# Level matmuls of a gated linear recurrence and value products of attention in column tiles of TensorE, and a later tanh

## Chip, core and metric

The kernel runs on one core of one Trainium2 chip. The metric is the device time of one execution in microseconds. A core has five engines with instruction streams of their own: TensorE (PE in the profile; its weight loads are PEld), VectorE (DVE), ScalarE (ACT), GpSimd (POOL) and SyncE (SP). Matmuls write to PSUM, which has eight banks here; everything else lives in SBUF.

## The reference

Two layers of an encoder trunk work on 512 positions of 1024 channels. Each layer normalises x, makes one wide input projection, runs three branches on it, merges them with gates, and ends with an MLP. What the change touches is in branch A and branch C:

```python
def step(state, inp):                       # branch A, chunks of positions, per head
    qt, kt, vt, bt = inp                    # bt: running sum of the log forget gates
    diff = bt[:, :, :, None, :] - bt[:, :, None, :, :]
    decay = jnp.exp(jnp.where(tri[:, :, None], diff, -jnp.inf))
    attn = jnp.einsum('nhtk,nhsk,nhtsk->nhts', qt, kt, decay)
    o_intra = jnp.einsum('nhts,nhsv->nhtv', attn, vt)
...
y_a = (rms_norm(o_a, a_norm[l]) * jax.nn.silu(a_g.astype(jnp.float32).reshape(o_a.shape)))
...
o = jnp.einsum('bnhgqk,bnkhd->bnqhgd', p.astype(v.dtype), vb)   # branch C, values
```

Branch A has 4 heads of 128 channels and runs forwards and backwards. Branch C is attention in a band of three blocks of 128 keys, with 8 query heads on 2 key and value heads of 64 channels.

## The kernel before, in words

All matrices are fp32. The big products are split into a rounded high and a low part and done as three matmuls (lines 268 to 270, 319 to 321, 532 to 534, 566 to 568). Weights come in chunks of 128x1024; ACT casts each chunk to its high part (`wh`, line 262) and DVE subtracts to get the low part (`wl`, line 263).

A layer has a stage in which branch A's heads, branch C and the remaining projections run beside each other. Python code gives the order of creation and priorities (`hp`, `later`, `overlap`); the scheduler of the framework then orders each engine's instructions by them and by its own estimate of times. `tc.issue_after(i)` holds an instruction back until `i` has been placed.

Branch A, `a_head`: the decay between positions t and s of a chunk is worked out by levels, L = 1, 2, 4, 8, 16, 32, 64. At a level the positions fall into blocks of L, and the decay between two neighbouring blocks is a product of a factor for the query (`qt`) and one for the key (`kt`), both made by an Exp on ACT from the running sums `ex`, which DVE extends level by level (line 775). So a level's share of the 128x128 matrix `at` (per group of 128 positions, of which there are four) is a plain product of `kt` and `qt`, right where the two blocks are neighbours and meaningless elsewhere. `attn` computes the whole 128x128 product for four groups into a PSUM tile of 128x512 (four matmuls, line 734). For L = 1 the tile is copied as it is (ACT, line 754); for L = 2 to 16 `put` copies it under a mask of the right entries (DVE, line 739, masks in `amask_t`), with one more product for the diagonal itself (`key` times `q`) at L = 2; for L = 32 and 64 the blocks off the diagonal are copied (ACT, line 767). In all there are 8 calls of `attn` for a head, and 4 heads in each of 2 layers. After the levels come the states (lines 779 to 807) and the product of `at` with the values (`av`, line 819).

Branch C, `c_out`: for a pair of heads `j` and a block of queries `n` the probabilities are transposed (`pT`, line 1209) and multiplied with the values `cv` (line 1214). The value tile has the 64 channels of both heads side by side, so one matmul per key block computes both heads' queries (256 columns) against both heads' channels (128 rows), and half of the result is used: two copies of 64 partitions (line 1216) take the right halves to `yc`.

`gate_a` projects branch A's output gate, scales it, and makes its SiLU from a tanh (lines 1109 to 1113) as soon as it can. The four gates are multiplied into branch A's heads at line 1280, ahead of the product `yA`. Branch C's `yc` is split into high and low parts (`yh`, line 327, and `yl`) ahead of the product `yC`.

Of the kernel before, what the change touches and what calls it, by code (L numbers as in the profile page):

```python
# [8 lines left out]
U8 = mybir.dt.uint8  # L9
# [3 lines left out]
P = 128  # L13
# [16 lines left out]
def ap_of(t, off, dims):  # L30
    return bass.AP(tensor=t.tensor, offset=t.offset + off, ap=[t.ap[0]] + dims)
# [47 lines left out]
def trunk(tc, x0v, xT, xt, ws, fnb, bsb, snk, wst, rope, cmask, amask, ident, out):  # L79
    nc = tc.nc  # L80
# [35 lines left out]
    def T(tag, name, dt=F32):  # L116
        where = part[HOME[tag]] if tag in HOME else sb
        return where.tile([P, S], dt, tag=tag, bufs=SLOTS[tag], name=nm(name))
# [161 lines left out]
    def proj(xs, name, *key, bank="m"):  # L280

        return proj_w(xs, name, wload(*key), bank=bank)
# [443 lines left out]
    def a_head(l, h, ex, q, vt, oa):  # L726

        at = part["br"].tile([P, 4, P], F32, tag="at", bufs=2, name=nm("at"))

        def attn(kk, qq):  # L730
            pt = PT("a", "at")
            for st in range(4):
                c = slice(st * P, (st + 1) * P)
                nc.tensor.matmul(pt[:, c], kk(st), qq[:, c], start=True, stop=True)  # L734
            return pt

        def put(pt, mi):
            mk = ap_of(amask_t, mi * P, [[0, 4], [1, P]])
            nc.vector.copy_predicated(at, mk, pt.rearrange("p (a b) -> p a b", a=4))

        X, R, Y, PP = 0, S, 2 * S, 3 * S
        for li, L in enumerate(LEVELS):
            nb = 256 // L
            shp = "p (b h i) -> p b h i"
            e_k = ap_of(ex, 0, [[2 * L, nb], [2 * S + L, 2], [1, L]])
            e_q = ap_of(ex, S, [[2 * L, nb], [2 * S + L, 2], [1, L]])
            qt = T("a", "qt")
            nc.scalar.activation(qt.rearrange(shp, b=nb, h=2), e_q, AF.Exp)  # L748
            nc.vector.tensor_tensor(qt, qt, q, ALU.mult)
            kt_ = T("a", "kt")  # L750
            nc.scalar.activation(kt_.rearrange(shp, b=nb, h=2), e_k, AF.Exp)
            if L == 1:
                pt = attn(lambda st: kt_[:, st * P:(st + 1) * P], qt)
                at_copy[0] = nc.scalar.copy(at, pt.rearrange("p (a b) -> p a b", a=4))
                dg = Z2("key")[:, 0]
                nc.scalar.activation(dg.rearrange(shp, b=nb, h=2), ap_of(ex, 2 * S, [[2, nb], [1 - 2 * S, 2], [1, 1]]), AF.Exp)
                nc.vector.tensor_tensor(dg, dg, kt_, ALU.add)
            else:
                pt = attn(lambda st: kt_[:, st * P:(st + 1) * P], qt)
                if L < 32:  # L760
                    put(pt, li)
                    if L == 2:
                        put(attn(lambda st: dg[:, st * P:(st + 1) * P], q), 0)
                else:
                    for r in range(0, P, L):
                        o = r ^ L
                        nc.scalar.copy(at[r:r + L, :, o:o + L], ap_of(pt[r:r + L], o, [[P, 4], [1, L]]))  # L767

            d = [[2 * L, nb], [1, L]]
            z = [[2 * L, nb], [0, L]]
            for o_, ostep, i_, istep in ((X, PP + L - X, PP + 2 * L - 1, -L), (Y + L, R - Y - L, R, L)):
                o_ap = ap_of(ex, o_, [[ostep, 2]] + d)
                nc.vector.tensor_tensor(o_ap, o_ap, ap_of(ex, i_, [[istep, 2]] + z), ALU.add)  # L775
            yield
# [130 lines left out]
    for l in range(DEPTH):  # L907
# [127 lines left out]
        begin("Y1")  # L1035
        begin("br")
        if l == 0:
            amask_t = cst.tile([P, 7 * P], U8, name="amask_t")
            for i in range(2):
                w = slice(i * 448, (i + 1) * 448)  # L1040
                am = T("a", "am")
                nc.sync.dma_start(am[:, 0:448], amask[:, w])
                nc.vector.tensor_copy(amask_t[:, w], am[:, 0:448])
            snk_t = const(bass.AP(tensor=snk.tensor, offset=snk.offset, ap=[[0, P], [1, 16]]), [P, 16], name="snk_t")
            nc.vector.tensor_scalar(snk_t, snk_t, -1.0, None, ALU.mult)
        cmask_t = part["br"].tile([P, 3 * P], F32, tag="cmask", bufs=1, name=nm("cmask"))
# [59 lines left out]
        sg = []  # L1106

        def gate_a():
            z = evac(proj(xs, "ag", l, "ag", len(sg)), "l2", "ag")
            th = T("jk", "th")  # L1110
            nc.scalar.activation(th, z, AF.Tanh, scale=0.5)
            nc.vector.scalar_tensor_tensor(z, th, 1.0, z, ALU.add, ALU.mult)
            sg.append(z)


        for t, view in ((cos_t, natural), (sin_t, sorted_)):
# [82 lines left out]
        def c_out(j, n, lo_, nb, Ps):  # L1199
# [11 lines left out]
            po = PT("s", "po")  # L1211
            for b in range(nb):
                kb = (lo_ + b) * P
                nc.tensor.matmul(po[:, 0:2 * P], cv[:, kb:kb + P], pT[:, b].rearrange("p a b -> p (a b)"), start=b == 0, stop=b == nb - 1)  # L1214
            for h, r in enumerate((lo64, hi64)):
                nc.scalar.copy(yc[j][r, n * P:(n + 1) * P], po[r, h * P:(h + 1) * P])

        def gates(tag, i, fl):

# [37 lines left out]
        with later(30000):  # L1257
            for h in range(4):
                gate_a()

            ys = y_split(yc, "yh")
            kept = []
            for fl in range(2):
                th = gates("ch", 0, fl)
# [273 lines left out]
def _host(x, w_in, ln1, lb_logits, a_norm, w_s, b_s, sink, w_br, w_out, ln2, w_up, w_down, final_norm):  # L1538
# [28 lines left out]
    cm[:, 2 * P:] = np.where(j <= i, 0.0, NEG)  # L1567
    a["cmask"] = cm
    am = [i == j]
    for L in LEVELS[1:7]:  # L1570
        am.append((i // (2 * L) == j // (2 * L)) & (i // L != j // L))
    a["amask"] = np.concatenate(am, axis=1).astype(f)
    a["ident"] = np.eye(P, dtype=f)
    return a

# [22 lines left out]
```

## Time and profile before

| what | value |
|---|---|
| median of 3 runs | 1606.75 us (1604.58 to 1606.84) |
| the profiled execution | 1605.07 us |
| its span | 1603.3 us |
| share of the clock granted to TensorE | 0.997 |
| stage of the mixers, layer 0 | about 160 to 430 us |
| stage of the mixers, layer 1 | about 978 to 1226 us |

The page gives the busy time of each engine, and the chain of work that ended last, followed back from the last instruction. Groups of instructions are given as line, engine, operation, tile written and tiles read, shapes, count, and then busy time, mean duration in ns, and the idle time of the engine just before them with the instruction that ended it. A timeline row gives the start, the time up to the end of the last one of a merged row, and a count; an engine's idle time before it stands in brackets. An fp32 matmul of the program is two records in the profile.

### The profile page before, as it was taken

How to read it: one execution, taken by the hardware profiler on the slowest of the kernel's cores; microseconds unless marked ns; L12 is line 12 of the kernel's file. 1: busy time of each engine (PE TensorE's matmuls, PEld its weight loads, DVE VectorE, ACT ScalarE, POOL GpSimd, SP SyncE). 2: the span in 40 equal slices, each digit the busy share in tenths (PEclk: the TensorE clock that was granted, in tenths of full speed). 3: DMA queues.
4: the chain of work that ended last, by engine and by line, in shares of the span. 5: the costliest groups of instructions: out<-in, count | busy, mean ns of one | idle time of the engine just before them, and what ended most of it. 6: DMA issues, size and time to landing. Idle time of an engine off the chain costs nothing.

```text
span 1603.3 us, 24656 instructions
## 1 busy us (share of the span) xinstructions
PE 1574.3 (98%) x9186; PEld 1420.6 (89%) x9186; DVE 1312.3 (82%) x1980; ACT 1065.4 (66%) x1819; POOL 185.1 (12%) x249
## 2 busy tenths in 40 slices
PE   9999999999999999999999999999999999999997
PEld 8887889899889999999888888799998898989896
DVE  7876898785677989797997769998856789797988
ACT  7667668686337848576876766688763477576675
POOL 1020000000231110100211100000003210110101
PEclk9999999999999999999999999999999999999999
DMA  9764321222485776866745742222225767867644
GB/s 348 196 164 128 123 74 65 89 96 92 154 293 158 190 194 182 200 182 178 191 132 172 219 137 82 79 73 86 86 87 203 244 187 193 205 174 201 173 110 112
DMA packets 74152, 250.55 MB, mean 156 GB/s; under 512 B 9168, under 2 KB 9552, under 8 KB 74032
## 3 DMA queue, kind: packets, MB, share of 16 engines
q1 hardware_dynamic: 45216, 156.03, 28.0%
q0 software_dynamic: 24064, 84.29, 24.0%
q10 hardware_dynamic: 4752, 8.65, 1.5%
q8 instruction: 72, 1.18, 0.3%
q14 instruction: 48, 0.39, 0.1%
HBM read 230.07 MB, written 18.87 MB: 155 GB/s over the span
## 4 chain that ended last, share of the span: by engine, by line
PE 79%; DVE 10%; ACT 5%; issue 3%; DMA 2%; POOL 1%; POOLq 0%; DVEq 0%; ACTq 0%
PE blks L534 3%; PE blks L533 3%; PE blks L532 3%; PE blkc L566 3%; PE blkc L567 3%; PE blkc L568 3%; DVE wl L263 3%; PE blka L534 2%; PE blka L533 2%; PE blka L532 2%; PE at L734 2%; PE po L1214 2%; PE blka L566 2%; PE blka L567 2%; PE blka L568 2%
## 5 line engine op out<-in xcount | busy, mean ns | idle before, releaser
L263 DVE TENSOR_TENSOR wl<-wr,wh 128x1024 fp32r<-128x1024 f32 x166 | 202.5, 1220 | 77.0 <-ACT wh L262 68.3
L262 ACT CAST wh<-wr 128x1024 fp32r<-128x1024 f32 x166 | 173.7, 1047 | 129.9 <-PE yA L320 27.9
L263 DVE TENSOR_TENSOR wl<-t,wh 128x1024 fp32r<-128x1024 f32 x158 | 192.0, 1219 | 52.2 <-ACT wh L262 51.6
L262 ACT CAST wh<-t 128x1024 fp32r<-128x1024 f32 x158 | 165.1, 1046 | 101.5 <-PE blks L533 24.0
L262 ACT CAST wh<-b 128x1024 fp32r<-128x1024 f32 x91 | 94.9, 1043 | 49.9 <-PE blks L533 14.0
L263 DVE TENSOR_TENSOR wl<-b,wh 128x1024 fp32r<-128x1024 f32 x91 | 110.6, 1219 | 16.0 <-ACT wh L262 15.4
L252 POOL DMA_DIRECT2D t<-in_ws_dram x72 | 65.4, 918 | 376.9 <-DMA t<-in_ws_dram 210.9
L533 PE MATMUL blks<-wh,sl 128*128 128x512 f32 x256 | 96.5, 380 | 1.2 <-DVE sl L328 1.2
L532 PE MATMUL blks<-wh,sh 128*128 128x512 f32 x256 | 93.3, 379 | 0.0
L534 PE MATMUL blks<-wl,sh 128*128 128x512 f32 x256 | 90.9, 381 | 0.2 <-DVE wl L263 0.2
L775 DVE TENSOR_TENSOR ex<-ex 128x512 f32<-128x512 f32 x112 | 78.9, 721 | 0.2
L328 DVE TENSOR_TENSOR sl<-u,sh 128x512 fp32r<-128x512 f32 x112 | 75.0, 682 | 2.0 <-ACT sh L327 2.0
L567 PE MATMUL blkc<-xl,wh 128*128 128x256 f32 x256 | 70.1, 275 | 0.0
L566 PE MATMUL blkc<-xh,wh 128*128 128x256 f32 x256 | 70.0, 275 | 0.0
L327 ACT CAST sh<-u 128x512 fp32r<-128x512 f32 x112 | 67.5, 614 | 3.6 <-DVE u L631 3.6
L568 PE MATMUL blkc<-xh,wl 128*128 128x256 f32 x256 | 69.6, 275 | 0.0
L252 POOL DMA_DIRECT2D wr<-in_ws_dram x32 | 28.0, 874 | 340.6 <-DVE t L501 92.8
L734 PE MATMUL at<-qt,kt 128*128 128x128 f32 x448 | 65.4, 276 | 1.7 <-DVE ex L775 1.5
L748 ACT ACTIVATE qt<-ex 128x512 f32<-128x512 f32 x56 | 37.6, 672 | 42.5 <-DVE ex L775 26.1
L734 PEld LDWEIGHTS at<-qt,kt 128*128 128x128 f32 x448 | 59.5, 192 | 4.2 <-ACT at L767 2.3
L533 PEld LDWEIGHTS blks<-wh,sl 128*128 128x128 f32 x256 | 48.4, 189 | 8.8 <-DVE sl L328 2.0
L534 PEld LDWEIGHTS blks<-wl,sh 128*128 128x128 f32 x256 | 48.4, 189 | 8.2 <-DVE wl L263 1.6
(444 smaller groups left out, 5316.7 us busy)
## 6 DMA issues: line engine op xcount, KB each, us to landing
wr<-in_ws_dram SPq DMA_DIRECT2D x134, 512.0 KB, 3.7
b<-in_ws_dram SPq DMA_DIRECT2D x91, 512.0 KB, 5.4
t<-in_ws_dram POOLq DMA_DIRECT2D x72, 512.0 KB, 8.3
t<-in_ws_dram SPq DMA_DIRECT2D x58, 512.0 KB, 4.4
wr<-in_ws_dram POOLq DMA_DIRECT2D x32, 512.0 KB, 5.6
thd<-zt ACTq DMA_DIRECT2D x32, 256.0 KB, 4.5
th<-thd POOLq DMA_DIRECT2D x32, 256.0 KB, 3.7
mgd<-mg POOLq DMA_DIRECT2D x16, 256.0 KB, 2.5
```

The source lines that it names most:

```text
L252: nc.gpsimd.dma_start(self.t[what][i], self.chunk(q, i), accum_op=ALU.add)
L262: cast_i[0] = nc.scalar.copy(hi, raw)
L263: sub_i[0] = nc.vector.tensor_tensor(lo, raw, hi.bitcast(F32), ALU.subtract)
L328: return nc.vector.tensor_tensor(lo, src, hi.bitcast(F32), ALU.subtract)
L532: nc.tensor.matmul(o, xh[:, t], h, start=start and k == 0, stop=False, skip_group_check=True)
L533: nc.tensor.matmul(o, xl[:, t], h, start=False, stop=False, skip_group_check=True)
L534: i = nc.tensor.matmul(o, xh[:, t], l_, start=False, stop=k == 3, skip_group_check=True)
L566: nc.tensor.matmul(o, hl[0][:, c], xh, start=start and k + j == 0, stop=False, skip_group_check=True)
L567: nc.tensor.matmul(o, hl[0][:, c], xl, start=False, stop=False, skip_group_check=True)
L568: i = nc.tensor.matmul(o, hl[1][:, c], xh, start=False, stop=k == 3, skip_group_check=True)
L734: nc.tensor.matmul(pt[:, c], kk(st), qq[:, c], start=True, stop=True)
L775: nc.vector.tensor_tensor(o_ap, o_ap, ap_of(ex, i_, [[istep, 2]] + z), ALU.add)
```

## The change

The level products of branch A are computed only in the blocks that are used. `attn` now takes a width `w`: for each of the four groups it makes 128 / w matmuls, each with w columns of `kt` as weights and w columns of `qt` (or `q`) as moving data. The result, w by w, goes to partitions r to r + w, which are also the column tile of TensorE (`tile_position=(0, r)`); the four groups lie side by side, so the PSUM tile has 4w columns. For L up to 16 and for the diagonal w is 32, and the results, the 32x32 blocks on the diagonal, are collected in the first 32 columns of `at` (`diag`). L = 32 and L = 64 take their blocks off the diagonal straight, with w = L. At L = 32 the three diagonal blocks below the first are copied to their places first. The masks shrink to 32 columns each, with 5 in place of 7.

Branch C's value products are made head by head: 64 columns of `cv` as weights, 128 queries as moving data, output at partitions 0 to 63 or 64 to 127 in the same 128 columns. One copy takes the result to `yc`.

The tanh of the output gates, and the product behind it, move from `gate_a` to a function `silu` that is called after `yc` has been split, and are held back until the last cast of that split (`halves_i[0]`) has been placed.

```diff
+        diag = at[:, :, 0:32]
+
-        def attn(kk, qq):
+        def attn(k_, q_, w, other):
+
             pt = PT("a", "at")
             for st in range(4):
-                c = slice(st * P, (st + 1) * P)
-                nc.tensor.matmul(pt[:, c], kk(st), qq[:, c], start=True, stop=True)
-            return pt
+                for r in range(0, P, w):
+                    k0 = st * P + r
+                    q0 = st * P + (r ^ w if other else r)
+                    nc.tensor.matmul(pt[r:r + w, st * w:(st + 1) * w], k_[:, k0:k0 + w], q_[:, q0:q0 + w], start=True, stop=True, tile_position=(0, r), skip_group_check=True)
+            return pt[:, 0:4 * w].rearrange("p (a b) -> p a b", a=4)
 
         def put(pt, mi):
-            mk = ap_of(amask_t, mi * P, [[0, 4], [1, P]])
-            nc.vector.copy_predicated(at, mk, pt.rearrange("p (a b) -> p a b", a=4))
+            nc.vector.copy_predicated(diag, ap_of(amask_t, mi * 32, [[0, 4], [1, 32]]), pt)
...
             if L == 1:
-                pt = attn(lambda st: kt_[:, st * P:(st + 1) * P], qt)
-                at_copy[0] = nc.scalar.copy(at, pt.rearrange("p (a b) -> p a b", a=4))
+                at_copy[0] = nc.scalar.copy(diag, attn(kt_, qt, 32, False))
...
+            elif L < 32:
+                put(attn(kt_, qt, 32, False), li)
+                if L == 2:
+                    put(attn(dg, q, 32, False), 0)
             else:
-                pt = attn(lambda st: kt_[:, st * P:(st + 1) * P], qt)
-                if L < 32:
-                    put(pt, li)
-                    if L == 2:
-                        put(attn(lambda st: dg[:, st * P:(st + 1) * P], q), 0)
-                else:
-                    for r in range(0, P, L):
-                        o = r ^ L
-                        nc.scalar.copy(at[r:r + L, :, o:o + L], ap_of(pt[r:r + L], o, [[P, 4], [1, L]]))
+                pt = attn(kt_, qt, L, True)
+                if L == 32:
+                    for r in range(32, P, 32):
+                        nc.scalar.copy(at[r:r + 32, :, r:r + 32], diag[r:r + 32])
+                for r in range(0, P, L):
+                    nc.scalar.copy(at[r:r + L, :, r ^ L:(r ^ L) + L], pt[r:r + L])
...
-            amask_t = cst.tile([P, 7 * P], U8, name="amask_t")
-            for i in range(2):
-                w = slice(i * 448, (i + 1) * 448)
-                am = T("a", "am")
-                nc.sync.dma_start(am[:, 0:448], amask[:, w])
-                nc.vector.tensor_copy(amask_t[:, w], am[:, 0:448])
+            amask_t = cst.tile([P, 5 * 32], U8, name="amask_t")
+            am = T("a", "am")[:, 0:5 * 32]
+            nc.sync.dma_start(am, amask)
+            nc.vector.tensor_copy(amask_t, am)
...
         def gate_a():
-            z = evac(proj(xs, "ag", l, "ag", len(sg)), "l2", "ag")
+            sg.append(evac(proj(xs, "ag", l, "ag", len(sg)), "l2", "ag"))
+
+        def silu(z, after):
             th = T("jk", "th")
-            nc.scalar.activation(th, z, AF.Tanh, scale=0.5)
+            with tc.issue_after(after.ins):
+                nc.scalar.activation(th, z, AF.Tanh, scale=0.5)
             nc.vector.scalar_tensor_tensor(z, th, 1.0, z, ALU.add, ALU.mult)
-            sg.append(z)
...
             for b in range(nb):
                 kb = (lo_ + b) * P
-                nc.tensor.matmul(po[:, 0:2 * P], cv[:, kb:kb + P], pT[:, b].rearrange("p a b -> p (a b)"), start=b == 0, stop=b == nb - 1)
-            for h, r in enumerate((lo64, hi64)):
-                nc.scalar.copy(yc[j][r, n * P:(n + 1) * P], po[r, h * P:(h + 1) * P])
+                for h, r in enumerate((lo64, hi64)):
+                    nc.tensor.matmul(po[r, 0:P], cv[:, kb + h * 64:kb + (h + 1) * 64], pT[:, b, h], start=b == 0, stop=b == nb - 1, tile_position=(0, h * 64), skip_group_check=True)
+            nc.scalar.copy(yc[j][:, n * P:(n + 1) * P], po[:, 0:P])
...
             ys = y_split(yc, "yh")
+            for z in sg:
+                silu(z, halves_i[0])
```

The scheduler then places the instructions anew. Three places show it. The first is PE in layer 0, where head 0 reaches its last two levels, beside the projection `gz` (a merge gate). Before:

```order
L269 MATMUL gz_2078<-xl_193,wh_2074 128x512
L734 MATMUL at_1477<-qt_1472,kt_1475 128x128 x4
L270 MATMUL gz_2078<-xh_192,wl_2075 128x512
L268 MATMUL gz_2078<-xh_196,wh_2074 128x512
L269 MATMUL gz_2078<-xl_197,wh_2074 128x512
```

The same place after the change:

```order
L270 MATMUL gz_2215<-xh_188,wl_2212 128x512
L739 MATMUL at_1546<-qt_1541,kt_1544 32x32 x10
L739 MATMUL at_1577<-qt_1572,kt_1575 64x64 x8
L739 MATMUL at_1546<-qt_1541,kt_1544 32x32 x6
L268 MATMUL gz_2215<-xh_192,wh_2211 128x512
```

Where one level stood as four wide matmuls, 16 narrow ones of L = 32 now stand with the 8 of L = 64 in their midst.

The second place is PE a little later, where head 0 ends with its product `av` while head 1 is at its level L = 8. Before:

```order
L819 MATMUL av_1972<-vt_677,at_1397 128x128
L734 MATMUL at_2133<-qt_2128,kt_2131 128x128
L819 MATMUL av_1972<-st_1845,qd_1849 128x128
L734 MATMUL at_2133<-qt_2128,kt_2131 128x128
L819 MATMUL av_1972<-st_1882,qd_1886 128x128
```

After:

```order
L821 MATMUL av_2108<-vt_677,at_1394 128x128
L739 MATMUL at_2270<-qt_2265,kt_2268 32x32
L821 MATMUL av_2108<-st_1945,qd_1949 128x128
L739 MATMUL at_2270<-qt_2265,kt_2268 32x32
L821 MATMUL av_2108<-st_2006,qd_2010 128x128
```

The alternation was there already, between products of one shape; now full and narrow matmuls take turns. In the whole of PE's new order there are 896 matmuls of 32x32, 64 of 64x64 and 160 of 64x128, and neighbours differ in output width (128, 64 or 32) 440 times.

The third place is ACT at the end of layer 1's stage, around the split of the last `yc`. Before:

```order
L1111 ACTIVATE th_11912<-ag_11910 128x512
L834 ACTIVATE on_11593<-oT_11588,x0v_t 128x512
L1216 COPY yc_11356<-po_11507 64x128 x2
L1111 ACTIVATE th_11948<-ag_11946 128x512
L327 CAST yh_11963<-yc_11356 128x512
L262 CAST wh_12165<-wr_12163 128x1024
```

After:

```order
L836 ACTIVATE on_12366<-oT_12361,x0v_t 128x512
L1218 COPY yc_12080<-po_12275 128x128
L327 CAST yh_12724<-yc_12080 128x512
L1114 ACTIVATE th_12728<-ag_12611 128x512
L1114 ACTIVATE th_12731<-ag_12644 128x512
L262 CAST wh_12938<-wr_12936 128x1024
```

The four tanh (`th`) now follow the cast `yh`, two of them ahead of the next weight cast.

More of the change, by code (lines that the diff above doesn't have):

```diff
@@ L1569, in _host @@
     am = [i == j]
-    for L in LEVELS[1:7]:
+    for L in LEVELS[1:5]:
         am.append((i // (2 * L) == j // (2 * L)) & (i // L != j // L))
-    a["amask"] = np.concatenate(am, axis=1).astype(f)
+    a["amask"] = np.concatenate([np.concatenate([m[r:r + 32, r:r + 32] for r in range(0, P, 32)]) for m in am], axis=1).astype(f)
     a["ident"] = np.eye(P, dtype=f)
```

## The prediction

> **What bounds the kernel now.** I read the page first: the busy times, then the chain that ended last.
>
> ```profile
> span 1603.3 us, 24656 instructions
> PE 1574.3 (98%) x9186; PEld 1420.6 (89%) x9186; DVE 1312.3 (82%) x1980; ACT 1065.4 (66%) x1819; POOL 185.1 (12%) x249
> ...
> PE 79%; DVE 10%; ACT 5%; issue 3%; DMA 2%; POOL 1%; POOLq 0%; DVEq 0%; ACTq 0%
> ```
>
> TensorE (PE) is busy in 98% of the span and holds 79% of the chain. So a matmul that goes away is worth nearly its own share of PE's stream, unless another engine is just behind. Next come the windows of the two mixer stages (one per layer) in which branches A and C run, and, inside each, the stretch where PE has gaps.
>
> ```profile
> core 0: us, PE busy (x) PEld busy (x) DVE busy (x) ACT busy (x) POOL busy (x), PEclk, DMA share, GB/s
> 160.00:430.00 270.00, 264.40 (x1488) 236.57 (x1487) 212.22 (x420) 184.55 (x404) 17.04 (x27) 0.99 0.26 90
> 978.00:1226.00 248.00, 241.63 (x1371) 216.73 (x1370) 202.73 (x408) 175.16 (x390) 17.24 (x27) 1.00 0.24 85
> ...
> 180.00:240.00 60.00, 56.43 (x314) 49.61 (x314) 59.44 (x105) 42.17 (x78) 1.10 (x2) 1.00 0.23 80
> 1000.00:1040.00 40.00, 36.07 (x207) 31.84 (x206) 37.66 (x71) 26.18 (x56) 1.11 (x2) 1.00 0.21 76
> ```
>
> Over a whole stage VectorE (DVE) has room: 212.2 of 270 us and 202.7 of 248. Only in the two short stretches is it full (59.4 of 60, 37.7 of 40), and there PE stands idle for 3.6 and 3.9 us. Everything the change touches lies in these stages; the MLP is untouched.
>
> **Part 1, the level matmuls of branch A.** The groups of PE, and how closely their instructions follow each other:
>
> ```profile
> L734 PE MATMUL at<-qt,kt 128*128 128x128 f32 x448 | 65.4, 276 | 1.7 <-DVE ex L775 1.5 <-ACT at L767 0.2
> L1214 PE MATMUL po<-pT,cvt 128*128 128x256 f32 x160 | 40.5, 379 | 0.0
> L734 PE MATMUL at<-q,key 128*128 128x128 f32 x64 | 8.5, 276 | 0.8 <-DVE at L739 0.8
> ```
>
> ```profile
> 179.70 1.05 PE L734 MATMUL at<-qt,kt 128*128 128x128 f32 x8
> 180.59 1.06 PE L734 MATMUL at<-q,key 128*128 128x128 f32 x8
> ...
> 418.88 1.03 PE L1214 MATMUL po<-pT,cvt 128*128 128x256 f32 x4
> ```
>
> The program has 256 matmuls for 448 + 64 = 512 records, so one fp32 matmul runs as two pieces, each with its own weight load. A call of the helper, four matmuls, is 8 pieces, and the next call starts 0.89 us later: 0.111 us a piece. There are 64 calls (8 heads times 8): 57.0 us of PE.
>
> After the change 56 calls are sixteen matmuls of 32x32 outputs, 32 pieces; the 8 calls of L = 64 are eight matmuls of 64x64, 16 pieces. Streaming shrinks: the old 0.111 us is for 128 moving columns, so 32 columns make 0.028 us and 64 make 0.056. But the pieces are four times (twice) as many. No column-tiled matmul is in this trace, so its price has to be bounded. From above: nothing smaller than a 128-column piece is seen in a row, and half of its price, 0.056 us, would hold if issuing loads and matmuls took that long. From below: four tiles that run side by side share 0.028 us, 0.007 each. The nearest row is the closest start of a load and a matmul after another one:
>
> ```profile
> 228.62 0.60 PE L1209 MATMUL pT<-id_t,sc 128*128 128x128 f32 x4
> 228.98 0.41 PE L1182 MATMUL sc<-k,q 128*128 128x384 f32 x1
> 229.22 0.33 PE L1182 MATMUL sc<-kl,q 128*128 128x384 f32 x1
> 229.39 0.38 PE L268 MATMUL yB<-yh,wh 128*128 128x512 f32 x1
> ...
> 228.95 0.19 PEld L1182 LDWEIGHTS sc<-k,q 128*128 128x128 f32 x1
> ```
>
> The last of the four transposes starts at about 228.95 (228.62 + 0.60 less one duration of 0.27); load and matmul of the next product start at 228.95 and 228.98. So a pair can be issued in 0.03 us, which is also what one 32-column piece streams. I take 0.03: 32 x 0.03 = 0.96 us a call, and 56 x (0.96 - 0.89) = **+3.9 us**. L = 64: 16 x 0.03 = 0.48, two tiles sharing 0.056; 8 x (0.48 - 0.89) = **-3.3 us**. So most of the expected halving is not in my sum: four times fewer columns are paid for with four times more pieces.
>
> **Part 2, the value products of branch C.** Four pieces of line 1214 last 1.03 us, each 0.379 long, so they start (1.03 - 0.379) / 3 = 0.217 us apart; 160 of them take 34.7 us. Now every key block has one matmul for each head instead of one for both: 64 output partitions, 128 moving columns, 320 pieces. One streams 0.111 us as above; two column tiles side by side make 0.056 each, 17.9 us; with no overlap 35.5. A piece of 128 columns is long against the 0.03 us of issue, so both tiles can be fed, and I take the overlap: **-16.8 us**; the other end is +0.8.
>
> **Part 3, switching between widths.** In PE's new order the output width (128, 64 or 32) changes 440 times between neighbours; before, never. In the rows above, transposes, plain fp32 and rounded fp32 products follow each other without a gap: 0.60 us of transposes, then the scores, then yB at 229.39. That is the nearest row, and by it a switch costs **0**. The upper end is a drained pipeline: a piece lasts 0.276 us and the next one starts after 0.111, so 0.165 us of each lies beyond its streaming; 440 x 0.165 = 72.6 us.
>
> The Trainium skill, "TensorEngine Tiling (Array Packing)", Key Properties, says that a change of the tiling mode, unlike a change of tile, drains TensorE. No run shown here has such a change; by that rule the switches are the term that decides, as in the first rival below.
>
> **Part 4, the copies behind them.**
>
> ```profile
> L739 DVE COPY_PREDICATED at<-amask_t,at 128x512 f32<-128x512 uint8 x40 | 29.3, 733 | 8.5 <-PE at L734 8.3
> ...
> L802 DVE SCALAR_TENSOR_TENSOR st<-st,ms,stp 128x128 f32<-128x128 f32 x32 | 10.9, 341 | 0.2
> ...
> L1216 ACT COPY yc<-po 64x128 f32<-64x128 f32 x64 | 16.5, 257 | 13.0 <-PE po L1214 12.5
> ...
> L767 ACT COPY at<-at 32x128 f32<-32x128 f32 x32 | 8.1, 254 | 0.8 <-PE at L734 0.5
> ...
> L754 ACT COPY at<-at 128x512 f32<-128x512 f32 x8 | 4.7, 584 | 0.9 <-PE at L734 0.9
> ```
>
> The 40 masked copies go from 512 to 128 columns. DVE's operation of that size from PSUM is line 802's, 0.341 us, so 40 x 0.39 = 15.7 us of DVE go. ScalarE (ACT): 8 copies of 0.584 become about 0.26 (-2.6), 64 copies of line 1216 become 32 of the same length (-8.2), 24 copies of the diagonal blocks come in at 0.254 (+6.1). ACT has slack all through the stage; costs nothing. The masked copies in the two full stretches:
>
> ```profile
> core 0: us, DVE busy (x), PEclk, DMA share, GB/s
> 180.00:240.00 60.00, 5.84 (x8) 1.00 0.23 80
> 1000.00:1040.00 40.00, 2.58 (x4) 1.00 0.21 76
> ```
>
> Twelve of them, 12 x 0.39 = 4.7 us off the engine that sets the pace there, against 7.5 us of PE idle time. PE's own stream in those stretches shrinks a little too, so I take **-3 us** (ends 0 and -4.7). The mask's load is one DMA in place of two and one cast in place of two, on SP and DVE ahead of the first masked copy; POOL keeps its instructions and swaps a few neighbours. Both cost nothing, under the work of the stage before.
>
> **Part 5, the gates' tanh.** The end of layer 1's stage:
>
> ```profile
> 1214.11 0.52 ACT L1216 COPY yc<-po 64x128 f32<-64x128 f32 x2
> 1214.65 0.63 ACT L1111 ACTIVATE th<-ag 128x512 f32<-128x512 f32 x1
> 1215.18 0.60 ACT L327 CAST yh<-yc 128x512 fp32r<-128x512 f32 x1
> ...
> 1215.84 1.13 PE L319 MATMUL yC<-wh,yh 128*128 128x512 f32 x4 [1.89 <-ACT yh L327]
> ...
> 1224.58 1.88 DVE L328 TENSOR_TENSOR yl<-on,yh 128x512 fp32r<-128x512 f32 x3
> ...
> 1228.68 0.38 PE L319 MATMUL yA<-wh,yh 128*128 128x512 f32 x1
> ```
>
> PE waits 1.89 us for the cast, and one tanh stands between the copy and it: moving it behind the cast is worth its 0.53 us here (1215.18 - 1214.65). The new wait queues four tanh, then four products on DVE, behind the cast; branch A's operands are late by at most 4 x 0.63 us. They are ready at 1226.5 and used from 1228.68, and the first only needs the first head, so 2.2 us cover it; without that cover it would cost some 2 us. I take **-0.5**.
>
> **Sum.** +3.9 - 3.3 - 16.8 + 0 - 3 - 0.5 = -19.7 us against the profiled execution of 1605.07 us (1.7 below the median of the runs shown, 0.1%): **1585 us**, 1.2% faster.
>
> **Rivals.**
> *The switches drain PE (slower).* Against it stands only that other changes of kind cost nothing; for it, that half-width outputs use the array in another way and that the new order interleaves single 32-wide products with full ones. At 0.165 us each it gives 1585 + 73 = 1658. It decides from 20 / 440 = 0.045 us a switch; at 0.1 us it gives 1629. The skill's rule above is this rival.
> *Issue is slower than 0.03 us when pairs come in rows (slower).* At 0.056 us a pair: 56 x (1.79 - 0.96) + 8 x (0.90 - 0.48) = +50, so 1635. For it: no row shows a run of such pairs. Against: the single pair at 228.95.
> *All four tiles run side by side (faster still).* At 0.007 us a piece the 56 calls take 12.5 us instead of 53.8: 1585 - 41 = 1544. For it: streaming is the only limit that the rows of 0.111 us show.
> The Trainium skill, "TensorE: Matmul & The Clock Gate", Part 3, gives tiles that start about 4 ns apart and finish together, which is this rival; no run shown here can test it.
> *Column tiles do not overlap (no change).* Then part 2 is +0.8 and L = 64 is 16 x 0.056 = 0.90, no gain: 1585 + 17.6 + 3.3 = 1606. The edit would do its arithmetic with a quarter of the array.
>
> **Chances.** Forecast 0.32; four tiles side by side 0.24; drained switches 0.26; slow issue 0.11; no overlap 0.07. Within 0.2% (3 us, about what a measurement of this kernel can tell from no change) is the last: faster 0.56, same 0.07, slower 0.37. The range runs from the full overlap, 1544, to 1645, which leaves out the top of the drain. The forecast's own range is 1565 to 1594, from half of the overlap in part 1 (-20) to half of part 2's gain missing (+8.4).
>
> **What would show it.** The start-to-start time of the 32x32 pieces: 0.03 by me, under 0.02 or over 0.05 by the rivals. Four pieces of a key block in branch C: 0.22 us by me, 0.43 before. The gap between a narrow matmul and its full neighbour: none by me; 0.1 us or more is the drain. DVE's busy time falls by some 16 us, and PE's idle time at 180 to 240 us and 1000 to 1040 goes down. A time above 1606 with short pieces and no gaps would mean that something outside PE, such as the order of heads against fills, was moved badly.

## The result, and the profile after

| kernel | median | range | runs | profiled execution | ratio to before |
|---|---|---|---|---|---|
| before | 1606.05 us | 1604.58 to 1606.84 | 4 | 1605.07 us | 1 |
| after | 1627.44 us | 1626.51 to 1629.54 | 4 | 1629.54 us | 1.0136 [1.0119, 1.0154] |

The change makes the kernel 1.4% slower. The head of the page of the changed kernel, and its chain that ended last:

```profile
span 1627.8 us, 27739 instructions
PE 1598.4 (98%) x10754; PEld 1399.8 (86%) x10754; DVE 1300.3 (80%) x1979; ACT 1062.0 (65%) x1811; POOL 186.2 (11%) x249
...
PE 78%; DVE 10%; DMA 4%; ACT 3%; issue 3%; POOL 1%; SPq 0%; POOLq 0%; DVEq 0%; ACTq 0%
```

PE still bounds the kernel with the same share, and the added 24.5 us of span are 24.1 us of PE's busy time. So PE streams fewer columns and is busy for longer. The groups of the narrow matmuls (line, engine, tiles, rows*columns of the array, shape, count; then busy time and the mean ns of one):

```profile
L739 PE MATMUL at<-qt,kt 128*32 128x32 f32 x1536 | 45.3, 201 | 2.9 <-ACT at L771 1.6 <-DVE qt L753 1.2
L1217 PE MATMUL po<-pT,cvt 128*64 128x128 f32 x320 | 38.9, 293 | 0.0
L739 PE MATMUL at<-qt,kt 128*64 128x64 f32 x128 | 10.9, 246 | 4.1 <-DVE qt L753 4.1
```

Two rows of before were `po` with 40.5 us and `at` with 65.4; neither has halved. The timeline of PE in the changed kernel shows why (start, length of a merged row, count), at a call of L = 1 and at one value product of branch C (two pieces):

```profile
167.62 1.05 PE L1075 MATMUL mx<-wst,bv 128*128 128x128 f32 x8
168.62 0.46 PE L739 MATMUL at<-qt,kt 128*32 128x32 f32 x32
169.00 1.16 PE L1075 MATMUL mx<-wst,bv 128*128 128x128 f32 x8
...
228.48 0.38 PE L270 MATMUL yB<-yh,wl 128*128 128x512 f32 x1
228.79 0.43 PE L1217 MATMUL po<-pT,cvt 128*64 128x128 f32 x2
229.15 0.48 PE L268 MATMUL yB<-yh,wh 128*128 128x512 f32 x1
229.47 0.38 PE L269 MATMUL yB<-yl,wh 128*128 128x512 f32 x1
229.69 0.38 PE L270 MATMUL yB<-yh,wl 128*128 128x512 f32 x1
```

First the call: 32 pieces fit into 0.46 us, of which one piece's own length is 0.20, so they start (0.46 - 0.20) / 31 = **0.008 us** apart. A piece of 32 columns streams 0.028 us, a quarter of 0.111, and a quarter of that is 0.007: all four column tiles run side by side. Then the switch: yB products follow each other every 0.216 us (229.47 to 229.69), but from the yB at 228.48 to the next narrow piece 0.31 us pass, and the first yB behind it holds the next up for 0.32. From 228.48 to 229.69 are 1.21 us; three yB make 0.65. The two pieces of `po` are one matmul for one head, and they start 0.16 us apart (0.43 - 0.27), with nothing in the other column tile. Counted as if they shared the array they stream 0.11, and 0.45 us are left over; streaming alone they take 0.22, and 0.34 us are left for one change to the narrow width and one back.

To add this up, I took every pair of neighbouring matmul records on PE, subtracted what the first of them streams (its columns, at the pace of undisturbed rows: 0.216 us a rounded 512-column product, 0.111 an fp32 piece of 128 columns, shared among the column tiles, so 0.008 for a piece of 32 columns as measured above), and sorted what is left by where it stands. "At changes of width" is the gap at the change and the one behind the first piece after it; numbers in us from the first to the last matmul, with counts in brackets. The two columns on the right are experiments that follow.

| | before | after | all_grouped | merged |
|---|---|---|---|---|
| streaming, full width | 1555.0 | 1462.9 | 1462.9 | 1462.9 |
| streaming, 32 and 64 wide | 0 | 35.8 | 35.8 | 35.8 |
| at changes of width | 0 | 71.8 (440) | 22.4 (163) | 17.4 (129) |
| small gaps elsewhere, under 0.4 us | 17.6 | 25.0 | 19.2 | 20.8 |
| waits over 0.4 us | 20.7 (16) | 22.8 (21) | 30.3 (23) | 31.3 (29) |
| sum | 1593.3 | 1618.2 | 1570.8 | 1568.1 |

The change saves 1555.0 - 1498.7 = 56.3 us of streaming, and pays 71.8 us for 440 changes of width, 0.163 us each, and 9.5 us of other gaps.

The streaming of 32 and 64 wide pieces is counted as if all column tiles were at work. Often they aren't: of the 249 runs of narrow matmuls in the changed kernel 135 are a single matmul, and 116 of the 320 pieces of `po` have no partner that starts within 0.03 us, against none in all_grouped. At 0.056 us each these 116 make 6.5 us as an estimate, which the table has among the changes of width and the small gaps.

### The profile page after: what moved, and what is told of

It reads as the page before. It is cut to its first block, busy times and chain, and to the rows that moved or that the text cites. A ratio compares the mean times of both kernels' runs of the same rounds, so it can differ in the third digit from the quotient of the medians.

```text
span 1627.8 us, 27739 instructions
## 1 busy us (share of the span) xinstructions
PE 1598.4 (98%) x10754; PEld 1399.8 (86%) x10754; DVE 1300.3 (80%) x1979; ACT 1062.0 (65%) x1811; POOL 186.2 (11%) x249
## 3 DMA queue, kind: packets, MB, share of 16 engines
q0 software_dynamic: 24064, 84.29, 24.1%
HBM read 229.69 MB, written 18.87 MB: 153 GB/s over the span
## 4 chain that ended last, share of the span: by engine, by line
PE 78%; DVE 10%; DMA 4%; ACT 3%; issue 3%; POOL 1%; SPq 0%; POOLq 0%; DVEq 0%; ACTq 0%
PE blks L534 3%; PE blks L533 3%; PE blks L532 3%; PE blkc L566 3%; PE blkc L568 3%; PE blkc L567 3%; DVE wl L263 3%; PE at L739 2%; PE blka L534 2%; PE blka L533 2%; PE blka L532 2%; PE po L1217 2%; PE wo L320 2%; PE wo L321 2%; PE wo L319 2%
## 5 line engine op out<-in xcount | busy, mean ns | idle before, releaser
L263 DVE TENSOR_TENSOR wl<-b,wh 128x1024 fp32r<-128x1024 f32 x91 | 111.0, 1224 | 15.9 <-ACT wh L262 13.6
L739 PEld LDWEIGHTS at<-qt,kt 128*32 128x32 f32 (+1 forms) x1664 | 36.4, 114 | 30.3 <-issue 8.2
L752 ACT ACTIVATE qt<-ex 128x512 f32<-128x512 f32 x56 | 37.7, 673 | 35.4 <-DVE ex L777 26.4
L739 PE MATMUL at<-qt,kt 128*32 128x32 f32 (+1 forms) x1664 | 53.5, 204 | 7.0 <-DVE qt L753 5.4
L1186 DVE CUSTOM_DVE_ANT_0 sc<-sc,cmask,snk_t 128x256 f32<-128x256 f32 (+1 forms) x64 | 35.0, 549 | 28.9 <-PE pT L1211 28.3
```

The costliest lines, as they stand in the source:

```text
L263: sub_i[0] = nc.vector.tensor_tensor(lo, raw, hi.bitcast(F32), ALU.subtract)
L739: nc.tensor.matmul(pt[r:r + w, st * w:(st + 1) * w], k_[:, k0:k0 + w], q_[:, q0:q0 + w], start=True, stop=True, tile_position=(0, r), skip ...
```

## The experiments

Three theories of the 71.8 us were set against each other. T1: each change of the output width costs PE a fixed time, wherever it stands. T2: the narrow pieces themselves cost it (their issue, their weight loads), whatever their neighbours. T3: neither; the new order of the instructions makes PE wait for other engines. Where a ratio is given, it is to the kernel before, measured on the same chip beside the run (medians of 1604.96 to 1606.05 us).

### One part at a time

The three parts of the change were made alone, each by undoing the other two in the changed kernel.

> Branch A's narrow level matmuls alone; branch C's value products and the tanh as before. PE's order has 324 changes of width, against 440 with the whole change. Theory 1 (each change of width costs PE some 0.18 us, all in: (21.4 + 56) / 440, with 56 us the streaming that goes if tiles run side by side): streaming -39, switches +57, so about 1624. Theory 2 (the narrow pieces themselves cost more than the wide ones they replace, wherever they stand): 1920 of the 2240 narrow pieces are here, so also about 1624; this run does not tell the two apart, but its half of the loss does, together with the next.

> Branch C's head-wise value products alone, 120 changes of width, everything else as before. Theory 1: streaming -17, switches 120 x 0.18 = +21, so about 1610. Theory 2: 320 of 2240 pieces, 1609. If column tiles did not overlap and switches were free: 1607.

> Only the output gates' tanh moved behind the cast of the last value tile. Prediction's term: -0.5 us, so 1605 to 1606. Rival: the products behind the tanh make branch A's operands late and PE waits some 2 us: 1608.

| alone | changes of width | median | ratio |
|---|---|---|---|
| a_only: level matmuls and their copies | 324 | 1626.73 us | 1.0136 [1.0111, 1.0160] |
| c_only: value products | 120 | 1608.47 us | 1.0021 [1.0009, 1.0033] |
| tanh: later tanh | 0 | 1604.04 us | 0.9997 [0.9985, 1.0009] |

Taken from 1605.42 us these are +21.3, +3.1 and -1.4, in sum +23.0, against +21.4 for all together. The loss is branch A's. The a_only trace is of its fastest execution (1619.63 us), 7 us under its median. In c_only the streaming falls by 17.0 us if every piece is counted as sharing the array, and 20.7 us go at 120 changes of width (0.17 each). But 96 of its 320 pieces have no partner, which at 0.056 us each is some 5 us of the halving that was not reached (an estimate); the rest is given back by the changes around it. The tanh alone makes no difference that can be measured.

### The same narrow matmuls, kept together

`a_grouped` and `all_grouped` leave every matmul as it is and change only where the scheduler may put it: a much higher priority for the narrow ones, the calls of a head in a chain, and the value products of the second head ahead of those of the first. The part for branch A (`later(-n)` raises the priority):

```diff
+GRP = 100000
...
+                    with later(-GRP), tc.issue_after(last_at[0].ins) if last_at[0] else contextlib.nullcontext():
-                    nc.tensor.matmul(pt[r:r + w, st * w:(st + 1) * w], k_[:, k0:k0 + w], q_[:, q0:q0 + w], start=True, stop=True, tile_position=(0, r), skip_group_check=True)
+                        i = nc.tensor.matmul(pt[r:r + w, st * w:(st + 1) * w], k_[:, k0:k0 + w], q_[:, q0:q0 + w], start=True, stop=True, tile_position=(0, r), skip_group_check=True)
+            last_at[0] = i
```

> Branch A's narrow matmuls alone, kept together call by call as in the grouped run: 118 changes of width, branch C and the tanh as before. Theory 1, with 0.18 us a change: 1605 - 39 + 21 = 1587, against 1627 for the same arithmetic with 324 changes. Theory 2 (price by pieces): no better than that run, 1625.

> The whole change, but the narrow matmuls of one call are kept together: a higher priority for them, the calls of a head in order, and the value products of a block of queries start only when both heads' probabilities are there. Same arithmetic, same 2240 narrow pieces, 163 changes of width in place of 440. Theory 1: 1606 - 56 + 163 x 0.18 = 1579, faster than before. Theory 2: no change against the whole change, about 1627. Theory 3 (the loss is in the order of heads and fills and in waits on other engines): between, with waits of PE instead of gaps at the switches.

Measured: a_grouped, 118 changes, 1597.56 us, 0.9950 [0.9931, 0.9968]; all_grouped, 163 changes, 1585.5 us, 0.9875 [0.9852, 0.9898]. The same 2240 narrow pieces cost 42 us less than in the changed kernel because they stand together. By T2 they would have cost the same. The groups of PE in all_grouped, and a run of value products in its timeline:

```profile
L742 PE MATMUL at<-qt,kt 128*32 128x32 f32 x1536 | 22.0, 199 | 4.0 <-ACT at L775 2.9 <-DVE qt L757 0.9
L1223 PE MATMUL po<-pT,cvt 128*64 128x128 f32 x320 | 24.6, 282 | 2.5 <-ACT pT L1216 2.5
```

```profile
229.11 0.38 PE L271 MATMUL yB<-yh,wl 128*128 128x512 f32 x1
229.42 0.66 PE L1223 MATMUL po<-pT,cvt 128*64 128x128 f32 x8
230.00 0.48 PE L269 MATMUL cq<-xh,wh 128*128 128x512 f32 x1
230.32 0.38 PE L270 MATMUL cq<-xl,wh 128*128 128x512 f32 x1
230.54 0.38 PE L271 MATMUL cq<-xh,wl 128*128 128x512 f32 x1
```

Line 739's 45.3 us of busy time are 22.0 here, and line 1217's 38.9 are 24.6, with the same counts. Eight `po` now stand where two did: 229.11 to 230.54 is 1.43 us, of which three wide products are 0.65 and eight `po`, now in both column tiles, 0.45. The 0.33 left over is paid once for eight pieces; in the changed kernel about as much (0.34) was paid for two, and those two streamed 0.22 because they stood alone.

T3 fails too: in the table above the waits over 0.4 us are 22.8 us in the changed kernel, only 2.1 more than before, and **more** in all_grouped (30.3), the faster one. They are what grouping gives back. T1's own numbers for these two, 1587 and 1579, were too low by 10.6 and 6.5 us, and the waits rose by 8.4 (a_only to a_grouped) and 7.5.

### A price for one change, and for one piece

Three probes add work to the kernel before. Ahead of each of 76 projections (in `proj_w`, behind `pt = PT(bank, name)`) stands a small matmul, whose result is overwritten. In probe_narrow2 it is one of 32x32, 2 pieces:

```diff
+        nc.tensor.matmul(pt[0:32, 0:32], id_t[:, 0:32], id_t[:, 0:32], start=True, stop=True, tile_position=(0, 0), skip_group_check=True)
```

In probe_narrow16 there are eight over the four tiles, 16 pieces:

```diff
+        for n in range(8):
+            r = 32 * (n % 4)
+            nc.tensor.matmul(pt[r:r + 32, 0:32], id_t[:, 0:32], id_t[:, 0:32], start=True, stop=True, tile_position=(0, r), skip_group_check=True)
```

In probe_full2 it has the full width and the same 32 moving columns, 2 pieces and no change of width:

```diff
+        nc.tensor.matmul(pt[:, 0:32], id_t, id_t[:, 0:32], start=True, stop=True, skip_group_check=True)
```

> The kernel before with one 32x32 matmul (2 pieces, its result overwritten at once) ahead of 76 of the projections: 152 changes of width and almost no work. It adds work that is thrown away, and nothing of the change. Theory 1: 152 x 0.18 = +27, about 1632. Theory 2: 152 pieces at 0.03 = +5, about 1610; at the 0.056 of the slow issue +9.

> The same with eight 32x32 matmuls in turn over the four column tiles (16 pieces) at each of the 76 places; where the scheduler puts other matmuls between, 238 changes of width in all. Theory 1: 238 x 0.18 + 1216 pieces x 0.008 = +53, about 1658, that is 26 more than with 2 pieces, 15 of it from the further changes. Theory 2: eight times the cost of 2 pieces, +40 to +70 over before and 35 to 60 over the run with 2.

> The same places with a full-width matmul of 32 moving columns (128 columns of weights, 2 pieces): no change of width. Its pieces wait for 128 columns of weights each, at most 0.11 us as in the wide rows: at most +17, 1605 to 1622. By theory 1 it costs less than the narrow probe although it loads four times the weights; by theory 2 more.

| probe | pieces | changes of width | median | ratio |
|---|---|---|---|---|
| probe_narrow2 | 152 | 152 | 1621.17 us | 1.0093 [1.0074, 1.0111] |
| probe_narrow16 | 1216 | 238 | 1640.43 us | 1.0214 [1.0196, 1.0231] |
| probe_full2 | 152 | 0 | 1619.62 us | 1.0080 [1.0058, 1.0103] |

By their times alone the probes are ambiguous: 152 narrow pieces cost 16.2 us and 152 full ones 14.7, so probe_narrow2 doesn't show by its time that the width matters. The timeline of probe_narrow2 shows what a change costs:

```profile
301.35 0.38 PE L270 MATMUL gz<-xh,wl 128*128 128x512 f32 x1
301.66 0.25 PE L287 MATMUL yB<-id_t 128*32 128x32 f32 x2
301.84 0.48 PE L268 MATMUL yB<-yh,wh 128*128 128x512 f32 x1
302.16 0.38 PE L269 MATMUL yB<-yl,wh 128*128 128x512 f32 x1
302.37 0.38 PE L270 MATMUL yB<-yh,wl 128*128 128x512 f32 x1
```

From 301.35 to 302.37 are 1.02 us, three wide products are 0.65, the two pieces some 0.02 if counted as shared: 0.35 us for two changes. They use one tile, so they stream 0.06, and 0.31 is the cost of the changes. Summed over the trace it is 27.7 us for 152 changes (0.18 each); but the waits over 0.4 us fall from 20.7 to 10.7 us in this kernel and the small gaps from 17.6 to 12.2, so only 13.6 us reach the span (16.2 by the medians).

probe_narrow16 is the clearer one, though its time was below both expectations: 35.5 us over before, where T1 had 53 and T2 40 to 70, and 19.3 over probe_narrow2, where T1 had 26 and T2 35 to 60. Its trace has 37.7 us at 238 changes, 0.158 each; its 1216 pieces stream 9.6 us, 0.008 each; the waits fall by 10.1. And probe_full2 shows that a short piece of full width has a price of its own, which the streaming of 32 columns (0.028 us) doesn't explain: 14.7 / 152 = 0.097 us a piece, against 0.008 for one of 32 columns' width among its like. That fits its expectation, by which a piece waits for its 128 columns of weights: in its trace the loads of two such pieces and the next stand at 305.59 and 305.70, 0.11 us apart.

In the changed kernel, the gaps sorted by kind of neighbours ("fp32" are the two-piece matmuls of full width, "rounded" the large products; us over the streaming, at the change and behind the first piece after it; counts):

```
                        at change   behind it    n
before  rounded > fp32    0.010       0.002     142
        fp32 > rounded   -0.084       0.087     141
after   full > 32         0.102       0.023     129
        full > 64         0.093       0.034      57
        32 > full         0.118       0.093     119
        64 > full         0.149       0.085      69
        32 <> 64          0.123       0.028      57
```

Between kinds of full width the two columns cancel: no price, as in the rows that the prediction quoted. Into a narrow width it is 0.13 us, back to the full one 0.21 to 0.23, from one narrow width to the other 0.15.

What this price is made of shows beside PE's weight loads (PEld). These are the loads of the changed kernel around the value product shown at its result:

```profile
228.27 0.19 PEld L270 LDWEIGHTS yB<-yh,wl 128*128 128x128 f32 x1
228.79 0.19 PEld L1217 LDWEIGHTS po<-pT,cvt 128*64 128x64 f32 x2 [0.33 <-issue]
229.15 0.19 PEld L268 LDWEIGHTS yB<-yh,wh 128*128 128x128 f32 x1 [0.17 <-issue]
229.26 0.19 PEld L269 LDWEIGHTS yB<-yl,wh 128*128 128x128 f32 x1
229.47 0.19 PEld L270 LDWEIGHTS yB<-yh,wl 128*128 128x128 f32 x1
```

Between products of full width a load starts with the matmul ahead of its own: the load at 229.26 is for the yB at 229.47. At a change of width it starts only together with its own matmul (228.79, 229.15), and both start 0.07 us before the end that the profile gives the matmul ahead (228.48 + 0.38 and 228.79 + 0.43). Of the 431 changes of this trace that have no wait over 0.4 us, 428 have these 0.070 us, within 0.002, whatever the two widths. So the matmul of the old width runs nearly to its end first, which costs 0.09 to 0.10 us beyond what it streams by itself in its own tile. Then the first matmul of the new width lasts longer, in step with the columns of weights that it loads: 0.48 in place of 0.38 us for 128 columns, 0.32 in place of 0.27 for 64, 0.22 in place of 0.20 for 32. A load that is no longer hidden fits this, and it is the difference by direction. (The ends of matmuls are modelled by the profile, so the 0.07 us is a distance to a modelled end; that it is the same everywhere is what counts. "At change" is 0.118 and 0.149 behind narrow matmuls because the table takes off only their share of streaming.)

### Fewer changes still

`merged` builds on all_grouped: a head's level products are collected over several levels and computed in four runs (after L = 2, 8, 32 and 64) into one PSUM tile. `merged300` does so with a weaker priority, `chain_only` is all_grouped with none (only the chain of calls and the order of the two heads are left), and `a_merged` is merged without the parts for branch C and the tanh.

```diff
+FLUSH = (2, 8, 32, 64)
...
-        def attn(k_, q_, w, other):
+        def attn(k_, q_, w, other, use):
+            calls.append((k_, q_, w, other, use))
...
+            if L in FLUSH:
+                flush()
```

The priority `GRP` is 300 in merged300 and 0 in chain_only, in place of 100000.

> The grouped version without the raised priority: calls of a head in order and the value products behind the second head's probabilities, 344 changes of width. Theory 1: from 163 to 344 changes, 181 x 0.107 to 0.163 = 19 to 30 us more than 1585.5, so 1605 to 1615. Theory 3 (waits made by the order): nearer to the grouped version, below 1600.

> The grouped version with the level products of a head collected into four runs (L = 1, 2 and the diagonal; 4 and 8; 16 and 32; 64), each into one PSUM tile: 129 changes of width against 163, the same 2240 narrow pieces. Theory 1 with the price that the traces so far give (0.107 us at the boundary in the probe, 0.163 with the second piece in the whole change): 34 x 0.107 to 0.163 = 4 to 6 us less than the grouped version's 1585.5, so 1580 to 1582. Rival: products that are held back make the copies and the next tiles late, and PE waits: 1586 or more.

> The same as the merged version with a priority raised by 300 instead of 100000: 148 changes of width. By the changes alone 2 to 3 us more than merged; if the strong priority is what makes PE wait (waits over 0.4 us add up to 30 us in the grouped version, 21 before), as much as 5 us less.

> Branch A alone, grouped and collected into four runs a head: 83 changes of width against 118. Theory 1: 35 x 0.107 to 0.163 = 4 to 6 us less than 1597.6, so 1592 to 1594. Compared with merged it shows what branch C's narrow products are worth when grouped: 17 us of streaming against 46 changes, 5 to 7.5 us: merged should be some 10 us faster than this.

| kernel | changes of width | at changes | waits over 0.4 us | median | ratio |
|---|---|---|---|---|---|
| chain_only | 344 | 51.2 us | 26.9 us | 1611.54 us | 1.0035 [1.0022, 1.0048] |
| merged300 | 148 | 20.3 us | 33.1 us | 1590.34 us | 0.9903 [0.9887, 0.9920] |
| merged | 129 | 17.4 us | 31.3 us | 1582.34 us | 0.9848 [0.9833, 0.9863] |
| a_merged | 83 | 11.8 us | 37.7 us | 1599.41 us | 0.9963 [0.9950, 0.9976] |
| a_grouped (above) | 118 | 16.5 us | 31.2 us | 1597.56 us | 0.9950 [0.9931, 0.9968] |

chain_only and merged came out as T1 had them (1605 to 1615, and 1580 to 1582). merged300 did not: it is 8.0 us above merged, where the changes made 2 to 3 and the weaker priority was to save up to 5. The price of a change is 0.135 to 0.149 us in all five. merged is the fastest kernel of this study: 1.5% under the kernel before and 2.8% under the changed one. a_merged missed its expectation by some 6 us: it saves 4.7 us at changes over a_grouped, as it should, and loses 6.5 in waits. merged is 17.1 us faster than it, where some 10 were expected of branch C. Where its PE waits (what waits, for what; us in total, times, longest):

```profile
PE yB L270 <- DVE gz L936: 5.1, 2, 3.2
PE po L1235 <- ACT pT L1231: 3.4, 5, 1.3
PE sc L1203 <- DVE q L1186: 3.3, 1, 3.3
...
PE at L748 <- DVE qt L777: 2.1, 2, 1.7
```

It is not the level products that wait longer (2.1 us on `qt`, against 5.3 in a_grouped) but the fills and branch C's work around them. Why their operands come later there was not tried. The page of merged, and PE's waits in it:

```profile
span 1577.6 us, 27745 instructions
PE 1541.4 (98%) x10754; PEld 1369.7 (87%) x10754; DVE 1295.3 (82%) x1979; ACT 1058.9 (67%) x1811; POOL 185.6 (12%) x249
...
PE 70%; DVE 16%; ACT 7%; issue 4%; DMA 3%; POOL 1%; POOLq 0%; ACTq 0%; DVEq 0%
```

```profile
PE yB L270 <- DVE gz L936: 4.2, 3, 1.9
PE at L748 <- DVE qt L777: 3.6, 3, 1.7
PE sc L1205 <- DVE mx L1207: 2.7, 2, 1.5
PE cq L270 <- DVE ck L1146: 2.0, 2, 1.3
```

PE's part of the chain is down from 78% to 70% and DVE's up from 10% to 16%: that points to VectorE's order in these stages as the next thing to try, and it was not tried. merged300 also has 26.2 us of small gaps, 5.4 more than merged. Its granted clock was 0.993 in the profiled execution and merged's 0.997; 0.4% of 1499 us of streaming makes 6 us as an estimate, enough for them, but no run sets the clock apart.

## Why the prediction was wrong

It gave 1585 us with a range of 1544 to 1645; measured were 1627.44, inside the range and on the other side of the kernel before. Step by step, in us against the kernel before:

| step | predicted | measured | from |
|---|---|---|---|
| 1: level matmuls, streaming | +0.6 | -39.2 | streaming in a_only, all tiles counted as busy; the 57.0 us are now 14.2 + 3.7 |
| 2: value products, streaming | -16.8 | -17.0 | streaming in c_only, both tiles counted as busy |
| 3: changes of width | 0 | +71.8 | 440 times 0.163 |
| 4: PE's waits, after lighter copies | -3 | +2.1 | waits over 0.4 us |
| 5: tanh | -0.5 | -2.4 to +1.4 | interval of the run alone, 0.9985 to 1.0009 of 1605 |
| small gaps elsewhere | none | +7.4 | the table of gaps |

Without the tanh the measured steps sum to +25.1, against 24.5 between the profiled executions.

**Part 3 is the step that failed.** It took the switch as free by the nearest row, in which transposes, fp32 and rounded products follow each other without a gap. That row was read rightly (the first two lines of the table by neighbours cancel), but none of its neighbours differs in width, so it could not bear on the question. What the runs show in its place is 0.163 us a change, 71.8 us in all: PE lets the old width run nearly to its end, and the weight load of the new one is not hidden. The upper end that the part named, 0.165 us a switch for a drained pipeline, is within 2% of that mean, and this closeness is partly luck: the drain takes 0.09 to 0.10 us of it, the loads and the tiles without a partner the rest, and in the other kernels the mean is 0.135 to 0.18. The order shown ahead of the prediction already had the 440 changes.

The Trainium skill, "TensorEngine Tiling (Array Packing)", Key Properties, says that a change of tiling mode drains TensorE while one of tile does not. The trace agrees on both: at a change of width the next matmul starts only 0.07 us before the modelled end of the one ahead, and in a run the four tiles take pieces 0.008 us apart.

**Part 1 was mis-sized, in the other direction.** Its price of 0.03 us a piece came from a load and a matmul that start 0.03 us behind another matmul, in a row of full-width pieces. By the table of neighbours such an early start (fp32 > rounded, -0.084 us) is paid back right behind it (0.087), so it was no rate of issue. Pieces of 32 columns start 0.008 us apart. The L = 64 calls, at 128 pieces in 3.7 us with both tiles at work, take 0.46 us a call, against 0.48 predicted. The rival "all four tiles run side by side" was true, and so was the rival "the switches drain PE": the prediction gave a chance to each alone, and none to both. Together they give 1585 - 41 + 73 = 1617; what is missing are the waits of part 4 (5.1 us from -3 to +2.1) and the 7.4 us of small gaps.

The Trainium skill, "TensorE: Matmul & The Clock Gate", Part 3, has tiles start about 4 ns apart. Here two products in the two column tiles of branch C start 6 to 7 ns apart; the 8 ns of the 32-column pieces lie near the 7 ns that four tiles need to stream them, so those do not test the figure.

**Part 2** was right where both heads' products stand together: in all_grouped eight pieces start (0.66 - 0.28) / 7 = 0.054 us apart, against the 0.056 forecast. It took for granted that the order keeps them together. In the changed kernel 116 of 320 pieces run with the other column tile empty, and what was gained is spent at the changes around them.

**Part 4:** the masked copies shrank, by more than I had worked out (12.2 us for 40, from 29.3; 17.1 against 15.7). In the two stretches where PE had gaps it did not help. The windows of before stand in the prediction; these are the same times in the changed kernel, with the copies' group:

```profile
L743 DVE COPY_PREDICATED at<-amask_t,at 128x128 f32<-128x128 uint8 x40 | 12.2, 305 | 32.2 <-PE at L739 31.9
```

```profile
core 0: us, PE busy (x) PEld busy (x) DVE busy (x) ACT busy (x) POOL busy (x), PEclk, DMA share, GB/s
...
180.00:240.00 60.00, 56.21 (x514) 46.00 (x513) 59.11 (x115) 43.35 (x83) 1.10 (x2) 0.97 0.28 89
1000.00:1040.00 40.00, 33.19 (x338) 26.90 (x337) 37.11 (x66) 27.89 (x57) 0.56 (x1) 0.96 0.24 74
```

DVE is as full as before (59.1 of 60 and 37.1 of 40 us), with 115 instructions where it had 105 in the first: the freed time went to other work of DVE, and PE's idle time went from 3.6 to 3.8 us and from 3.9 to 6.8 (layer 1's stage runs later here, so this second pair is not the same work). All of DVE's busy time fell by 12.0 us, not by 15.7.

**Part 5:** the wait that it spoke of did shrink. In the changed kernel the last `yC` waits for its cast as follows, where before it waited 1.89 us:

```profile
1240.17 1.13 PE L319 MATMUL yC<-wh,yh 128*128 128x512 f32 x4 [1.00 <-ACT yh L327]
```

That would be worth 0.9 us; alone it is below what the runs tell from no change.

The 7.4 us of small gaps were no term of the prediction. Sorted by kind, those between full-width matmuls do not grow; the growth lies inside the runs of narrow ones: 4.6 us among the products of `po`, 2.2 among the 32 wide and 1.0 among the 64 wide products of branch A. For `po` it is 1.0 us in all_grouped, where no piece lacks a partner. A lower clock, 0.995 in this execution against 0.997 before, is not needed for them.

## What to carry to other kernels

Before narrow column tiles go into a stream of full-width matmuls, count in the new order how often the width of neighbours changes, and set that count times a price (here 0.135 to 0.18 us) against the streaming saved. Count too how many narrow matmuls would stand alone, because they leave the other tiles empty. Here the tiles paid off as soon as they stood in runs (1627 to 1582 us with the same matmuls), and turned into a loss where a scheduler sprinkled them singly. A row in which things follow each other without a gap prices a new kind of neighbour only if it differs in the same property.

## What was not expected of the hardware

- Four 32-column tiles take a new fp32 piece every 0.008 us, weight load included, while a full-width piece with the same 32 moving columns cost 0.097 us in its probe, close to the 0.11 us by which its weight loads follow each other.
- A change of width is not symmetric: 0.13 us into a narrow width, 0.21 to 0.23 back to the full one, of which 0.09 appear only behind the first full-width piece. The weight load at a change starts with its own matmul, not with the one ahead.
- From 32 to 64 columns and back costs 0.15 us as well, although neither is the full width.
